# Weight sums of the second feed-forward layer as in-place adding transfers

## The chip, the cores and the metric

The kernel runs on one core of one Trainium2 chip. The metric is the device time of one execution in microseconds (us). The kernel before took 1249.65 us, the median of three runs that lie between 1248.87 and 1249.77 us.

## The reference, cut to what matters

One step of a decoder trunk of two layers: 512 prompt tokens and 64 sample tokens, width 1024, everything in float32. Layer 0 is a recurrent block, layer 1 windowed attention; each is followed by the feed-forward part that the change is about:

```
D_MODEL, D_FF = 1024, 2816
def swiglu(h, w_in, w_out):
    gate, up = jnp.split(h @ w_in, 2, axis=-1)
    return (jax.nn.silu(gate) * up) @ w_out
...
        h = modulate(rms_norm(x, norm_g[l, 1]), sh2, sc2)
        x = x + g2[:, None, :] * swiglu(h, ffn_w_in[l], ffn_w_out[l])
```

## The kernel before

**Halves and products.** The 576 tokens are handled as two halves of 288 columns, h = 0 and 1. A float32 product is made of three matmuls on operands that are split in a rounded part (`hi`, made by a cast on ScalarE) and the rest (`lo`, made by a subtraction on VectorE). `wh` are the ten buffers for split weights, `raw` the four buffers (512 KB each, 128 x 1024) into which weights are loaded by SyncE's queue, `h` the split input of the layer, `mm` the six PSUM banks.

**Pairs.** D_FF = 2816 is 22 blocks of 128 columns. The first three blocks of a layer (`PLAIN`) are computed directly. For each of the other 19 the gate's and the up projection's weight tile (a pair of `raw` tiles) are taken together as a 2 x 2 matrix of quarters r11, r12 (the gate tile's halves over the inner dimension) and r21, r22 (the up tile's), each 128 x 512, and the two halves of tokens as the other factor's columns. A Strassen scheme then needs seven products in place of eight: `11`, `12`, `22` take a plain quarter, `S1` to `S4` take sums of quarters. One product is 4 x 3 = 12 matmuls of 128x128 on 288 columns, a pair is 84.

**What stands where.** `steps(i)` gives seven closures for pair i; each calls `operand`, which claims a `wh` buffer, forms the sums that the product needs in place in the `raw` quarters (on VectorE), casts (ScalarE) and subtracts (VectorE). `todo` holds these closures in order, `pump` runs them as soon as `wh` buffers are left. `seven(i, name)` issues a product's matmuls and what follows them on PSUM. `raw.done()` gives a tile back, after which the next load may fill it. The blocks come in groups of 6, 6, 6 and 4 (the three plain ones are in the first); after a group its rows of `ffn_w_out` follow: `out(k, m, h)`, 8 x 2 products of 18 matmuls for a group of six.

**What sets the order.** Every call is recorded, and `Recorder.schedule` sorts all instructions of the whole program with costs of its own, then gives each engine its list, which that engine works off strictly in order. For a transfer issued by GpSimd (POOL) it reckons 1.02 us of issue, 0.65 us, 4 bytes per element at 345 bytes/ns, and 1.70 us, so 4.13 us from issue to landing for 128 x 512 floats. `reserve` says how many buffers of a kind must stay free when a tile is claimed out of turn; for `mm` it is 0.

The sums before, for one pair (r's are overwritten as they go):

```
S1:  r22 = r21 + r22
S2:  r21 = r11 - r21 ; r11 = r11 - r22
S4:  r12 = r12 - r11            (S3 takes r21)
```

Of the kernel before, what the change touches and what calls it, by code (L numbers as in the profile page):

```python
# [12 lines left out]
F32 = mybir.dt.float32  # L13
# [3 lines left out]
ALU = mybir.AluOpType  # L17
AX = mybir.AxisListType

P = 128  # L20
# [7 lines left out]
HC = 288  # L28
# [106 lines left out]
class Recorder:  # L135
    def __init__(self, shadow):
        self.shadow = shadow
        self.ops = []
        self.hist = {}
        self.kind_of = {}  # L140
        self.kinds = {}
        self.order = {}
        self.bias = 0
        self.hold = []
        self.batch = None
# [14 lines left out]
    def tile(self, pool, kind, cap, reserve, shape, dt, name):  # L160
        sh = self.shadow[kind in ("mm", "ada")].tile(shape, dt, tag=name, bufs=1, name="shadow_" + name)
        t = Sym(Ref(lambda: pool.tile(shape, dt, tag=kind, bufs=cap, name=name)), sh)
        n = sh.tensor.name
        self.kind_of[n] = kind
        self.kinds[kind] = (cap, reserve)
        self.order.setdefault(kind, []).append(n)
        return t

# [50 lines left out]
    def schedule(self):  # L219
# [35 lines left out]
        def alloc_time(op, now):  # L255
            t = 0.0
            need = {}
            for n in op.allocs:
                if n in got:
                    continue  # L260
                k = self.kind_of[n]
                sl = slots[k]
                i = need.get(k, 0)
                need[k] = i + 1
                o = self.order[k]
                while nxt[k] < len(o) and (o[nxt[k]] in got or o[nxt[k]] not in used):
                    nxt[k] += 1

                j, at = nxt[k], i
                while at and j + 1 < len(o):  # L270
                    j += 1
                    at -= o[j] not in got and o[j] in used
                m = i + (o[j] != n) * self.kinds[k][1]
                if len(sl) <= m:
                    return None
                t = max(t, sorted(sl)[m])
            return t
# [213 lines left out]
def trunk_kernel(ctx, tc, a):  # L491
# [10 lines left out]

    cnt = [0]

    def ps(pool=pmm, tag="mm"):
        cnt[0] += 1
        return rec.tile(pool, tag, NMM if tag == "mm" else (8 - NMM), RMM if tag == "mm" else 1, [P, 512], F32, f"{tag}{cnt[0]}")

    def aux():
        return ps()  # L510
# [401 lines left out]
    def quarters(c):  # L912

        if c == 0:
            kinds = [tb] * 8 + [ta] * 3 + [sl] * 13
            X2["kinds"] = kinds
            for j in (2, 3, 4):
                X2[j] = [None] * 4
        b11, b21, b12, b22 = [V2[h][k] for h, k in ((0, c), (0, c + 4), (1, c), (1, c + 4))]

        def two(j, y):
            X2[j][c] = [X2["kinds"].pop(0)(F32R) for _ in range(2)]
            split(X2[j][c][0].r[:, 0:HC], X2[j][c][1].r[:, 0:HC], y.f[:, 0:HC])
            y.done()

        def minus(o, p, q):
            V.tensor_tensor(*[y.f[:, 0:HC] for y in (o, p, q)], ALU.subtract)

        minus(b11, b12, b11)
        minus(b12, b22, b12)  # L930
        two(3, b12)
        minus(b22, b22, b11)
        minus(b21, b21, b22)
        two(2, b22)
        two(4, b21)

# [281 lines left out]
    def ffn(l, g, after):  # L1218
# [35 lines left out]
        todo = deque()  # L1254
        H2 = 4 * P

        def operand(i, name, src, sums=()):
            w = W[i, name] = whs()
            for o, p, q, op in sums:
                V.tensor_tensor(o, p, q, op)  # L1260
            S.copy(w.r[:, 0:H2], src)
            V.tensor_tensor(w.r[:, H2 : 2 * H2], src, w.f[:, 0:H2], ALU.subtract)

        def steps(i):

            ug_, uu = pairs_[i]

            def views():
                if uu.raw is None:
                    load_more()  # L1270
                return [u.raw.f[:, o : o + H2] for u in (ug_, uu) for o in (0, H2)]

            def a11():
                operand(i, "11", views()[0])

            def a22():
                operand(i, "22", views()[3])

            def s1():
                r11, r12, r21, r22 = views()  # L1280
                operand(i, "S1", r22, [(r22, r21, r22, ALU.add)])

            def s2():
                r11, r12, r21, r22 = views()
                operand(i, "S2", r11, [(r21, r11, r21, ALU.subtract), (r11, r22, r11, ALU.subtract)])

            def a12():
                operand(i, "12", views()[1])

            def s3():  # L1290
                operand(i, "S3", views()[2])
                uu.raw.done()
                nconv[0] += 1

            def s4():
                r11, r12, r21, r22 = views()
                operand(i, "S4", r12, [(r12, r12, r11, ALU.subtract)])
                ug_.raw.done()
                nconv[0] += 1

            return {"11": a11, "22": a22, "S1": s1, "S2": s2, "12": a12, "S3": s3, "S4": s4}

        def queue():
            for k, bs in enumerate(blocks):
                for i in range(max(PLAIN, sum(GROUPS[:k])), sum(GROUPS[: k + 1])):
                    st = steps(i)
                    if i == PLAIN:
                        nxt = steps(i + 1)
                        for s_, names in ((st, ("11", "12")), (nxt, ("11", "12")), (st, ("22", "S1", "S2", "S3", "S4")), (nxt, ("22", "S1", "S2", "S3", "S4"))):
                            for n in names:  # L1310
                                todo.append((1, s_[n]))
                    elif i > PLAIN + 1:
                        for n in ("11", "22", "S1", "S2", "12", "S3", "S4"):
                            todo.append((1, st[n]))
                for _ in {id(u) for u in outs[k][1]}:
                    todo.append((2, convert))
# [17 lines left out]
        def seven(i, name):  # L1334

            pump(lambda: (i, name) in W)
            w = W.pop((i, name))
            bank, ops = {"11": ("a", "B11"), "12": ("a", "B21"), "S1": ("e", "T1"), "S2": ("b", "T2"), "S3": ("b", "T3"),
                         "22": ("b", "T4"), "S4": ("e", "B22")}[name]
            b = B.setdefault(i, {})  # L1340
            if bank not in b:
                b[bank] = ps()
            o = b[bank][:, 0:HC]
            first = name in ("11", "S1", "S2")
            for k, (xh, xl) in enumerate(right(ops)):
                hi, lo = [w.r[:, q + k * P : q + (k + 1) * P] for q in (0, H2)]
                T.matmul(o, hi, xh, start=first and k == 0, stop=False, skip_group_check=True)
                T.matmul(o, hi, xl, start=False, stop=False, skip_group_check=True)
                T.matmul(o, lo, xh, start=False, stop=k == 3, skip_group_check=True)
            w.done()  # L1350
            pump()
            if name == "11":
                b["p1"] = ta()
                S.copy(b["p1"].f[:, 0:HC], o)
            elif name == "S1":
                b["p5"] = td()
                S.copy(b["p5"].f[:, 0:HC], o)
            elif name == "S2":

                V.tensor_tensor(o, o, b["p1"].f[:, 0:HC], ALU.add)  # L1360
                b["p1"].done()
                b["u2"] = td()
                S.copy(b["u2"].f[:, 0:HC], o)
            elif name == "12":

                b["g"] = ta()
                S.activation(b["g"].f[:, 0:HC], o, AF.Silu)
            elif name == "S3":

                y = b["p5"].f[:, 0:HC]  # L1370
                V.tensor_tensor(y, o, y, ALU.add)
            elif name == "22":

                y = b["g"].f[:, 0:HC]
                V.tensor_tensor(y, y, o, ALU.mult)
                whole(0, i, b["g"])
                del B[i]
            else:

                y, z = b["u2"].f[:, 0:HC], b["p5"].f[:, 0:HC]  # L1380
                V.tensor_tensor(y, o, y, ALU.add)
                S.activation(y, y, AF.Silu)
                G.tensor_tensor(z, y, z, ALU.mult)
                b["u2"].done()
                whole(1, i, b["p5"])
# [25 lines left out]
        def emit():  # L1411
            if l == 1:
                cache_out()
            queue()
            n_ = 0
            for k in range(len(GROUPS)):
                if k == 1 and l == 0:
# [30 lines left out]
                                ada_pace(1)  # L1448
                if k < len(GROUPS) - 1:
                    seven(n_, "11")  # L1450

        return emit

# [589 lines left out]
```

## Time and profile before

| what | value |
|---|---|
| median of three runs | 1249.65 us |
| span of the profiled execution (first to last instruction) | 1247.8 us |
| granted TensorE clock over the span | 0.994 |
| busy, of the span: TensorE / VectorE / ScalarE / GpSimd | 98% / 72% / 53% / 21% |
| moved by all transfers | 165.37 MB, mean 133 GB/s |

The span is that of one profiled execution; the page gives no other time for it, and the median lies 1.85 us above it. The second feed-forward layer runs from about 799 to 1238 us. Engine names in the profile: PE is TensorE, DVE VectorE, ACT ScalarE, POOL GpSimd, SPq and POOLq the queues of SyncE and GpSimd. All operations are recorded by one helper, so that all lines are L456 before and L458 after, and groups are told apart by tiles: `wh<-raw` is the making of a weight operand, `raw<-raw` a sum of quarters. "mean ns of one" is the time of one instruction; "idle before" is the time in which the engine stood still ahead of a group, with what ended it.

### The profile page before, as it was taken

The numbers are of one execution on the slowest core, as the hardware profiler recorded it, in microseconds if no ns is written. First come the engines' busy times: TensorE is split into PE (matmuls) and PEld (weight loads), VectorE is DVE, ScalarE is ACT, GpSimd is POOL, SyncE is SP. The second block draws the span as 40 slices with busy tenths as digits, with TensorE's granted clock in tenths as the row PEclk, the third lists the DMA queues.
The fourth block names the chain that finished last, engine by engine and source line by source line (L and its number), as shares of the span: only waits on it lengthen the run. The fifth ranks groups of instructions, "written<-read, shape, count | busy, mean of one in ns | idle before, by whom it ended". The sixth has DMA issues, their size and how long they took to land.

```text
span 1247.8 us, 25059 instructions
## 1 busy us (share of the span) xinstructions
PE 1225.9 (98%) x9468; PEld 1166.2 (93%) x9468; DVE 903.7 (72%) x2143; ACT 655.9 (53%) x1492; POOL 256.8 (21%) x542
## 2 busy tenths in 40 slices
PE   6999999999999999999999999999999999999997
PEld 4999999899999999999999888999999999999997
DVE  6789875984587467656779777658857856875776
ACT  4877773854155235423567578448523542552442
POOL 3455442100200110011034435100011011001011
PEclk8999999999999999999999999999999999999998
DMA  9966654434564654754612321422332332332322
GB/s 329 313 203 219 189 176 127 158 93 145 170 186 155 201 171 133 220 168 119 183 38 58 69 65 34 118 82 98 104 116 69 93 111 69 101 91 80 102 68 76
DMA packets 214507, 165.37 MB, mean 133 GB/s; under 512 B 23502, under 2 KB 197546, under 8 KB 214355
## 3 DMA queue, kind: packets, MB, share of 16 engines
q1 hardware_dynamic: 213938, 163.45, 43.0%
q8 instruction: 74, 1.21, 0.4%
q0 software_dynamic: 448, 0.32, 0.1%
q14 instruction: 47, 0.38, 0.1%
HBM read 160.85 MB, written 4.87 MB: 133 GB/s over the span
## 4 chain that ended last, share of the span: by engine, by line
PE 91%; ACT 3%; DVE 3%; DMA 2%; issue 1%; POOL 0%; SPq 0%; ACTq 0%; DVEq 0%; POOLq 0%
PE mm L456 86%; PE ada L456 5%; ACT ta L456 1%; DMA wh<-in_ada_w_dram 1%; ACT tb L456 1%; DMA raw<-in_rnn_w_in_dram 1%; DVE tb L456 0%; DVE h L456 0%; ACT h L456 0%; DVE sl L456 0%; DVE ta L456 0%; DVE wh L456 0%; SPq L456 0%; DVE acc L456 0%; ACT sl L456 0%
## 5 line engine op out<-in xcount | busy, mean ns | idle before, releaser
L456 PE MATMUL mm<-h,wh 128*128 128x288 f32 x4128 | 587.8, 297 | 1.5 <-ACT h L456 0.7
L456 PEld LDWEIGHTS mm<-h,wh 128*128 128x128 f32 x4128 | 558.4, 188 | 9.8 <-ACT h L456 2.5
L456 PE MATMUL mm<-sl,wh 128*128 128x288 f32 x3218 | 459.9, 296 | 0.0
L456 PEld LDWEIGHTS mm<-sl,wh 128*128 128x128 f32 x3218 | 436.6, 188 | 5.9 <-issue 3.4
L456 ACT CAST wh<-raw 128x512 fp32r<-128x512 f32 (+2 forms) x380 | 268.0, 722 | 325.2 <-PE mm L456 212.2
L456 DVE TENSOR_TENSOR wh<-raw,wh 128x512 fp32r<-128x512 f32 (+2 forms) x380 | 308.1, 825 | 73.5 <-ACT wh L456 50.1
L456 DVE SCALAR_TENSOR_TENSOR x<-mm,mods,x 128x256 f32<-128x256 f32 x160 | 76.9, 481 | 112.3 <-PE mm L456 112.2
L456 POOL TENSOR_TENSOR td<-td,td 128x288 f32<-128x288 f32 x38 | 35.5, 933 | 467.2 <-ACT td L456 461.1
L456 POOL TENSOR_TENSOR x<-x,ta 128x32 f32<-128x32 f32 x152 | 57.6, 380 | 309.2 <-DVE ta L456 309.1
L456 PE MATMUL mm<-tb,wh 128*128 128x288 f32 (+1 forms) x488 | 88.3, 297 | 0.0
L456 PEld LDWEIGHTS mm<-tb,wh 128*128 128x128 f32 x488 | 72.4, 188 | 1.9 <-DVE ta L456 0.8
L456 ACT COPY td<-mm 128x288 f32<-128x288 f32 (+2 forms) x140 | 49.0, 364 | 32.8 <-PE mm L456 16.8
L456 DVE TENSOR_TENSOR raw<-raw,raw 128x512 f32<-128x512 f32 x76 | 59.2, 779 | 0.5
L456 PE MATMUL mm<-ta,wh 128*128 128x288 f32 (+1 forms) x254 | 55.8, 297 | 0.0
L456 DVE TENSOR_TENSOR td<-mm,td 128x288 f32<-128x288 f32 x76 | 34.5, 454 | 25.9 <-PE mm L456 25.5
L456 ACT ACTIVATE ta<-x 128x288 f32<-128x288 f32 x56 | 24.4, 443 | 54.2 <-POOL x L456 51.1
L456 DVE TENSOR_TENSOR raw<-raw 128x512 f32<-128x512 f32 x76 | 52.1, 686 | 1.1
L456 PEld LDWEIGHTS mm<-ta,wh 128*128 128x128 f32 x254 | 41.7, 188 | 0.2
L456 PE MATMUL ada<-reg,cz 128*32 128x512 f32 (+1 forms) x304 | 36.1, 538 | 0.0
L456 ACT ACTIVATE ta<-ta,stat 128x256 f32<-128x256 f32 (+2 forms) x72 | 32.4, 475 | 7.0 <-DVE stat L456 6.8
L456 DVE TENSOR_TENSOR acc<-acc,ta 128x288 f32<-128x288 f32 x54 | 25.0, 464 | 13.6 <-ACT ta L456 13.3
L456 ACT CAST sl<-ta 128x288 fp32r<-128x288 f32 x54 | 23.2, 431 | 20.6 <-DVE ta L456 18.2
(201 smaller groups left out, 1195.0 us busy)
## 6 DMA issues: line engine op xcount, KB each, us to landing
raw<-in_ffn_w_in_dram SPq DMA_DIRECT2D x88, 512.0 KB
reg<-in_ada_w_dram SPq DMA_DIRECT2D x50, 512.0 KB
wh<-in_ada_w_dram SPq DMA_DIRECT2D x38, 512.0 KB
raw<-in_ffn_w_out_dram SPq DMA_DIRECT2D x48, 384.0 KB
raw<-in_rnn_w_in_dram SPq DMA_DIRECT2D x16, 512.0 KB
reg<-in_kv_ada_w_dram SPq DMA_DIRECT2D x10, 512.0 KB
raw<-in_rnn_w_out_dram SPq DMA_DIRECT2D x8, 512.0 KB
raw<-in_ffn_w_out_dram SPq DMA_DIRECT2D x8, 512.0 KB
```

Of the source, the lines that this page charges most:

```text
L456: self.rec.add(eng, lambda: getattr(obj, name)(*map(real, args), **{k: real(v) for k, v in kw.items()}), cost, outs, ins, func, lat, port, ...
```

## The change

The scheme is rewritten so that every sum of quarters is an addition into one of its own operands. The right factor's sums and the use of the products in PSUM take the signs that this leaves. In layer 0 the additions stay on VectorE (`plus` with l == 0), four per pair as before. In layer 1 each becomes a transfer issued from GpSimd with `accum_op=ALU.add`: 128 x 512 floats (256 KB) from one quarter added onto another, 76 in all for 19 pairs. The new sums of a pair, with the numbers that the prediction gives them:

```
(1) r11 += r21     after operand 11 has read r11
(2) r21 += r22     after (1)                      -> S1 reads r21
(3) r22 += r11     after (1), (2) and operand 22  -> S2 reads r22
(4) r12 += r22     after (3) and operand 12       -> S4 reads r12;  S3 reads r11, after (1)
```

The up tile is given back after (4), S1 and S2, the gate tile after S3 and S4. Two negations per pair (products `S3` and `22`) become scalar_tensor_tensor with a factor of -1 in place of tensor_tensor, in both layers, and so do two of the four differences of `quarters`. Last, in layer 1 the PSUM tiles `mm` are recorded with a reserve of 1 in place of 0 (`rmm`, `kept`).

```
+        def plus(o, p):
+            if l == 0:
+                V.tensor_tensor(o, o, p, ALU.add)
+            else:
+                G.dma_start(o, p, accum_op=ALU.add)
...
             def a22():
-                operand(i, "22", views()[3])
+                r11, r12, r21, r22 = views()
+                operand(i, "22", r22)
+                plus(r11, r21)
+                plus(r21, r22)
+                plus(r22, r11)
+                last_sum("22")
...
             def s2():
-                r11, r12, r21, r22 = views()
-                operand(i, "S2", r11, [(r21, r11, r21, ALU.subtract), (r11, r22, r11, ALU.subtract)])
+                operand(i, "S2", views()[3])
+                last_sum("S2")
...
+            def last_sum(name):
+                said.add(name)
+                if said >= {"22", "12"} and "sum" not in said:
+                    said.add("sum")
+                    plus(views()[1], views()[3])
+                if said >= {"sum", "S1", "S2"} and "up" not in said:
+                    said.add("up")
+                    uu.raw.done()
...
                 y = b["p5"].f[:, 0:HC]
-                V.tensor_tensor(y, o, y, ALU.add)
+                V.scalar_tensor_tensor(y, o, -1.0, y, ALU.mult, ALU.subtract)
...
+            rmm[0] = l
```

How this moves instructions is shown at two pairs in the middle of the layer, whose tiles are raw148 (gate) and raw149 (up), then raw150 and raw151. First VectorE before: three of the four sums of the first pair stand between its subtractions, and the fourth follows two rows on.

```order
L456 TENSOR_TENSOR wh401_12529<-raw149_12284,wh401_12529 128x512
L456 TENSOR_TENSOR x1_65<-x1_65,ta375_12536 128x32
L456 TENSOR_TENSOR raw149_12284<-raw149_12284 128x512
L456 TENSOR_TENSOR raw149_12284<-raw148_12232,raw149_12284 128x512
L456 TENSOR_TENSOR wh402_12556<-raw149_12284,wh402_12556 128x512
L456 TENSOR_TENSOR raw148_12232<-raw149_12284,raw148_12232 128x512
L456 TENSOR_TENSOR wh403_12579<-raw148_12232,wh403_12579 128x512
L456 TENSOR_TENSOR wh404_12585<-raw148_12232,wh404_12585 128x512
L456 TENSOR_TENSOR wh405_12592<-raw149_12284,wh405_12592 128x512
```

They are gone from VectorE, and POOL's list has them now. The same pair and the next one there, after the change, up to the first transfer of the two pairs that follow:

```order
L458 DMA raw148_12248<-raw149_12284 128x512
L458 DMA raw150_12515<-raw151_12534 128x512
L458 DMA raw149_12284<-raw149_12284 128x512
L458 DMA raw151_12534<-raw151_12534 128x512
L458 DMA raw149_12284<-raw148_12248 128x512
L458 TENSOR_TENSOR td137_12566<-td138_12590,td137_12566 128x288
L458 DMA raw151_12534<-raw150_12515 128x512
L458 DMA raw148_12248<-raw149_12284 128x512
L458 DMA raw150_12515<-raw151_12534 128x512
L458 TENSOR_TENSOR td139_12710<-td140_12756,td139_12710 128x288
L458 DMA raw152_12765<-raw153_12781 128x512
```

The two pairs' transfers alternate, (1) (1) (2) (2) (3) (3) (4) (4), and the gate-times-up product of the first pair (`td137`) stands among them. Over the whole layer the 19 pairs stand in 13 such runs: six runs of two pairs and, mostly where a group of blocks begins or ends, seven of one. ScalarE, in the list before, works the seven casts of the first pair (wh400 to wh406) nearly in a row, ahead of those of the second:

```order
L456 CAST wh400_12484<-raw148_12232 128x512
L456 CAST wh401_12529<-raw149_12284 128x512
L456 COPY ta376_12551<-mm451_12527 128x288
L456 CAST wh402_12556<-raw149_12284 128x512
L456 COPY td137_12570<-mm452_12548 128x288
L456 CAST wh403_12579<-raw148_12232 128x512
L456 CAST wh404_12585<-raw148_12232 128x512
L456 CAST wh405_12592<-raw149_12284 128x512
L456 ACTIVATE ta377_12607<-mm451_12527 128x288
```

In the list after, at the same place, the casts of the second pair (wh407, wh408, wh411, wh412) stand between those of the first, and S1's (wh402) comes behind six others:

```order
L458 CAST wh404_12570<-raw148_12248 128x512
L458 CAST wh407_12584<-raw150_12515 128x512
L458 COPY td138_12590<-mm453_12563 128x288
L458 ACTIVATE ta377_12603<-mm451_12523 128x288
L458 CAST wh408_12607<-raw151_12534 128x512
L458 COPY ta378_12621<-mm454_12599 128x288
L458 CAST wh405_12625<-raw148_12248 128x512
L458 CAST wh411_12639<-raw150_12515 128x512
L458 CAST wh412_12656<-raw150_12515 128x512
L458 CAST wh402_12663<-raw149_12284 128x512
```

So ScalarE's list, which also holds the copies out of PSUM (`ta<-mm`, `td<-mm`), now waits at several places for a transfer to land.

More of the change, by code (lines that the diff above doesn't have):

```diff
@@ L141, in __init__ @@
         self.kinds = {}
+        self.kept = {}
         self.order = {}
@@ L165, in tile @@
         self.kinds[kind] = (cap, reserve)
+        self.kept[n] = reserve
         self.order.setdefault(kind, []).append(n)
@@ L272, in alloc_time @@
                     at -= o[j] not in got and o[j] in used
-                m = i + (o[j] != n) * self.kinds[k][1]
+                m = i + (o[j] != n) * self.kept[n]
                 if len(sl) <= m:
@@ L503, in trunk_kernel @@
     cnt = [0]
+    rmm = [RMM]
     def ps(pool=pmm, tag="mm"):
         cnt[0] += 1
-        return rec.tile(pool, tag, NMM if tag == "mm" else (8 - NMM), RMM if tag == "mm" else 1, [P, 512], F32, f"{tag}{cnt[0]}")
+        return rec.tile(pool, tag, NMM if tag == "mm" else (8 - NMM), rmm[0] if tag == "mm" else 1, [P, 512], F32, f"{tag}{cnt[0]}")
     def aux():
@@ L927, in minus, with negated @@
             V.tensor_tensor(*[y.f[:, 0:HC] for y in (o, p, q)], ALU.subtract)
-        minus(b11, b12, b11)
+        def negated(o, p, q):
+            o, p, q = [y.f[:, 0:HC] for y in (o, p, q)]
+            V.scalar_tensor_tensor(o, p, -1.0, q, ALU.mult, ALU.subtract)
+        minus(b11, b11, b12)
         minus(b12, b22, b12)
         two(3, b12)
-        minus(b22, b22, b11)
-        minus(b21, b21, b22)
+        negated(b22, b22, b11)
+        negated(b21, b22, b21)
         two(2, b22)
@@ L1255, in ffn, with operand @@
         H2 = 4 * P
-        def operand(i, name, src, sums=()):
+        def plus(o, p):
[3 more added lines that the diff above has]
+                G.dma_start(o, p, accum_op=ALU.add)
+        def operand(i, name, src):
             w = W[i, name] = whs()
-            for o, p, q, op in sums:
-                V.tensor_tensor(o, p, q, op)
             S.copy(w.r[:, 0:H2], src)
@@ L1271, in views @@
                 return [u.raw.f[:, o : o + H2] for u in (ug_, uu) for o in (0, H2)]
+            said = set()
+            def last_sum(name):
[6 more added lines that the diff above has]
+                    uu.raw.done()
+                    nconv[0] += 1
+                if said >= {"S3", "S4"}:
+                    ug_.raw.done()
+                    nconv[0] += 1
             def a11():
@@ L1276, in a22 @@
             def a22():
-                operand(i, "22", views()[3])
+                r11, r12, r21, r22 = views()
[4 more added lines that the diff above has]
+                last_sum("22")
             def s1():
-                r11, r12, r21, r22 = views()
-                operand(i, "S1", r22, [(r22, r21, r22, ALU.add)])
+                operand(i, "S1", views()[2])
+                last_sum("S1")
             def s2():
-                r11, r12, r21, r22 = views()
-                operand(i, "S2", r11, [(r21, r11, r21, ALU.subtract), (r11, r22, r11, ALU.subtract)])
+                operand(i, "S2", views()[3])
+                last_sum("S2")
             def a12():
                 operand(i, "12", views()[1])
+                last_sum("12")
             def s3():
-                operand(i, "S3", views()[2])
-                uu.raw.done()
-                nconv[0] += 1
+                operand(i, "S3", views()[0])
+                last_sum("S3")
             def s4():
[L1296 to L1299, printed above, removed]
+                operand(i, "S4", views()[1])
+                last_sum("S4")
             return {"11": a11, "22": a22, "S1": s1, "S2": s2, "12": a12, "S3": s3, "S4": s4}
@@ L1370, in seven @@
                 y = b["p5"].f[:, 0:HC]
-                V.tensor_tensor(y, o, y, ALU.add)
+                V.scalar_tensor_tensor(y, o, -1.0, y, ALU.mult, ALU.subtract)
             elif name == "22":
                 y = b["g"].f[:, 0:HC]
-                V.tensor_tensor(y, y, o, ALU.mult)
+                V.scalar_tensor_tensor(y, o, -1.0, y, ALU.mult, ALU.mult)
                 whole(0, i, b["g"])
@@ L1450, in emit @@
                     seven(n_, "11")
+            rmm[0] = RMM
         return emit
```

## The prediction

> **What bounds the kernel now.** I first read the page's busy times, then the chain of waits in order of time, since it tells which engine ends each stage. The second feed-forward layer, the only place where transfers replace work, is one row of it:
>
> ```profile
> PE 1225.9 (98%) x9468; PEld 1166.2 (93%) x9468; DVE 903.7 (72%) x2143; ACT 655.9 (53%) x1492; POOL 256.8 (21%) x542
> ...
> 798.85 439.12 PE mm L456 x3311
> 1237.99 0.48 DVE x L456
> ```
>
> From 798.85 to 1237.99 us the chain never leaves PE. Then the windows, and the matmuls of that stretch by shape:
>
> ```profile
> 900.00:1000.00 100.00, 100.00 (x757) 100.00 (x756) 71.69 (x139) 42.68 (x86) 11.84 (x20) 1.00 0.33 96
> 820.00:860.00 40.00, 40.00 (x300) 39.39 (x299) 28.18 (x72) 25.33 (x63) 3.49 (x9) 1.00 0.35 113
> 940.00:980.00 40.00, 40.00 (x304) 40.00 (x303) 30.88 (x60) 18.50 (x39) 4.01 (x6) 1.00 0.28 80
> L456 PE MATMUL mm<-h,wh 128*128 128x288 f32 x1499 | 209.9, 296 | 0.1
> L456 PE MATMUL mm<-sl,wh 128*128 128x288 f32 x1417 | 204.7, 296 | 0.0
> ```
>
> The columns of a window are length, then busy us (and instructions) of PE, PEld, DVE, ACT, POOL, the granted clock, the share of the DMA engines, GB/s. PE starts 757 matmuls in 100 us at clock 1.00, one every 132.1 ns, and its idle time ahead of 2916 matmuls is 0.1 us. A pair's 84 matmuls take 84 x 132.1 ns = 11.1 us, an output part of 16 x 18 matmuls 38.0 us. VectorE, at 0.72, waits for PE. What VectorE loses here shortens nothing by itself.
>
> **What is taken away: 76 additions on VectorE.** The groups of 800 to 1237 us:
>
> ```profile
> L456 DVE TENSOR_TENSOR wh<-raw,wh 128x512 fp32r<-128x512 f32 (+2 forms) x170 | 129.6, 776 | 23.0 <-ACT wh L456 22.1
> L456 DVE TENSOR_TENSOR raw<-raw,raw 128x512 f32<-128x512 f32 x38 | 31.5, 830 | 0.2
> L456 DVE TENSOR_TENSOR raw<-raw 128x512 f32<-128x512 f32 x38 | 26.0, 687 | 0.5
> L456 ACT CAST wh<-raw 128x512 fp32r<-128x512 f32 (+2 forms) x170 | 113.8, 683 | 164.7 <-PE mm L456 95.2 <-DVE raw L456 41.9 <-issue 27.4
> ```
>
> 31.5 + 26.0 = 57.5 us of VectorE go, and with them the 41.9 us for which the casts waited for a sum. Both lie beside a PE that does not stand still. Worth: 0. The most that could be hidden in PE's even row is the difference between its best and its mean pace: 304 matmuls per 40 us are 131.6 ns each, the chain's 3311 take 132.6; 3311 x 1.0 ns = 3.3 us.
>
> **Signs, reserve, order.** 76 results in PSUM (two per pair, both layers) become scalar_tensor_tensor. The nearest rows:
>
> ```profile
> L456 DVE TENSOR_TENSOR td<-mm,td 128x288 f32<-128x288 f32 x38 | 17.3, 454 | 10.8 <-PE mm L456 10.8
> L456 DVE SCALAR_TENSOR_TENSOR x<-mm,mods,x 128x256 f32<-128x256 f32 x75 | 36.1, 481 | 62.1 <-PE mm L456 62.1
> ```
>
> 481 ns on 256 columns is at most 541 on 288, 87 more than 454; 76 x 87 ns = 6.6 us over both layers, on VectorE, which waits 62.1 us for PE in that one group of the second layer alone. The 16 negated differences (of `quarters`) add at most 16 x 87 ns = 1.4 us, on the same engine. Worth: 0; the cover is VectorE's waiting for PE, and if that were used up, the copies out of PSUM would be late next. In layer 0 the four additions per pair stay. The reserve and the new order put the same products in another sequence on PE; between -1 and +3 us, and I take +0.5: one missed matmul slot (0.13 us) at each of the four turns from pairs to outputs.
>
> **What is put in: 76 transfers of 256 KB, in series.** No transfer with an addition is in this trace, nor one from SBUF to SBUF. The nearest are POOL's own transfers in a stretch where the DMA engines are otherwise quiet, and one weight load:
>
> ```profile
> 229.25 1.14 POOL L456 DMA_DIRECT2D out_sample_conv_dram<-raw  x2
> 230.38 0.53 POOL L456 DMA_DIRECT2D out_prompt_conv_dram<-raw  x1
> 229.00:230.25 1.25, 1.25 (x11) 1.04 (x10) 0.95 (x4) 0.72 (x2) 1.11 (x3) 1.00 0.00 0
> 230.25:231.50 1.25, 1.25 (x12) 1.25 (x11) 1.25 (x5) 0.35 (x2) 1.25 (x4) 1.00 0.38 93
> 0.00:50.00 50.00, 39.03 (x372) 31.62 (x373) 32.28 (x101) 29.30 (x66) 15.74 (x39) 0.93 1.01 342
> DMA to landing us min/median/max: 1.9/2.9/3.9
> DMA to landing us min/median/max: 3.8/5.1/5.9
> 915.31 68.45 SPq L456 DMA_DIRECT2D raw<-in_ffn_w_in_dram  x12
> 915.00:916.25 1.25, 1.25 (x12) 1.25 (x11) 1.02 (x3) 0.12 (x1) 0.00 (x0) 1.00 0.00 0
> 916.25:917.50 1.25, 1.25 (x11) 1.25 (x11) 0.58 (x2) 0.00 (x0) 0.18 (x1) 1.00 0.67 196
> 917.50:918.75 1.25, 1.25 (x12) 1.25 (x11) 0.12 (x1) 0.20 (x1) 0.07 (x1) 1.00 0.74 223
> 918.75:920.00 1.25, 1.25 (x11) 1.25 (x11) 1.05 (x3) 0.63 (x1) 0.25 (x1) 1.00 0.00 0
> ```
>
> POOL is occupied 0.57 us by an issue (1.14 for two); the first bytes move 1.0 us after it (229.25, and 0 GB/s until 230.25). From issue to landing the two 48 KB transfers took 1.9 to 3.9, median 2.9 us (the first landing row); those at the program's start, of at most 48 KB with the DMA engines full (share 1.01 in the first 50 us, 342 GB/s), 3.8 to 5.9 (the second). The weight load of 512 KB, issued at 915.31, moves its bytes between 916.25 and 918.75: 210 GB/s with its run-up.
>
> L, from issue to landing of one addition: the 208 KB beyond 48 KB at 210 GB/s add 1.0 us to the median 2.9, so 3.9 us. The low end is 1.9 + 0.65 = 2.55 (the same bytes at about 330 GB/s, near the 342 of the first 50 us); the high end 3.9 + 1.0 + 1.25 = 6.15, if the quarter that is added onto has also to be read through the same engines at 210 GB/s. I take 3.9: the stretch has a DMA share of 0.33, nearer to the quiet rows than to the full ones.
>
> How long may L be? Transfers (1) to (4) of a pair wait for each other, two pairs alternate, and the next two pairs' tiles are loaded when these are given back. So one run on POOL's list costs: load to last byte 3.4 us (915.31 to 918.75 at most), its second tile 1.6 (0.52 MB at 330 GB/s), a cast 0.62 and a subtraction 0.69 (rows below) before (1), 4 L, and a cast and subtraction behind (4): 7.6 + 4 L.
>
> ```profile
> L456 ACT CAST wh<-raw x170: 605/622/1056, 803.2 to 1201.8; 128x512 fp32r<-128x512 f32 x133, 128x768 fp32r<-128x768 f32 x24, 128x1024 fp32r<-128x1024 f32 x13
> L456 DVE TENSOR_TENSOR wh<-raw,wh x170: 677/692/1473, 804.4 to 1203.5; 128x512 fp32r<-128x512 f32 x133, 128x768 fp32r<-128x768 f32 x24, 128x1024 fp32r<-128x1024 f32 x13
> ```
>
> PE has 2 x 11.1 = 22.2 us of work for it: L may be (22.2 - 7.6)/4 = 3.65. Over a group of six pairs, four runs share 6 x 11.1 + 38.0 = 104.6 us: (26.15 - 7.6)/4 = 4.64, if the output part's own weights cost the buffers nothing. I put the limit in the middle, 4.15 us. With L = 3.9 the transfers are hidden, by a quarter of a microsecond. Beyond the limit each microsecond costs up to 13 runs x 4 = 52 us, since ScalarE's list stops at the cast that waits (S1's behind (2), S2's behind (3)), behind it the copies that empty PSUM, and behind those PE; POOL's list stops too, with the `td` products that the output part needs. SyncE's next loads come only after (4).
>
> A sentence of the Trainium skill speaks against my 3.9: "Collectives: The Full Stack", section "The bandwidth ceiling", says that an addition in the DMA engines needs two source reads on the same ring, which halves its rate. No run here shows it yet; by it the second read's 1.25 us would be added, L = 5.15 and (5.15 - 4.15) x 52 = 52 us more than before.
>
> **Sum.** Against the profiled execution: span 1247.8 + 0 (VectorE) + 0 (signs) + 0.5 (order) + 0 (transfers, hidden) = 1248.3 us. The median of the runs lies 1.85 us above this span; with it 1250.1 us. About 0.2% (2.5 us) is what a measurement of this kernel can tell from no change.
>
> **Rivals.**
>
> *Landings longer than the cover (slower).* Everything as above, with L from 4.2 us up. It decides where L passes 4.15; at 4.65 it costs 26 us (1276), at 5.15 52 us (1302), at 6.15 104 us (1354). For it speaks that 3.65 to 4.64 straddles my own L, that pairs alternate, so two additions share the DMA engines, and that the start's landings took 3.8 to 5.9 us. Against: they stood in a DMA share of 1.01, and the 0.33 here is mostly loads that wait for (4) themselves.
>
> *POOL kept from issuing by VectorE (slower).* POOL's own products in this layer vary:
>
> ```profile
> L456 POOL TENSOR_TENSOR td<-td,td x19: 802/1034/1344, 896.4 to 1205.8; 128x288 f32<-128x288 f32 x19
> ```
>
> From 0.80 to 1.34 us: a neighbour costs up to 0.54 us. If an issue suffers the same, L = 4.44 and (4.44 - 4.15) x 52 = 15 us, 1265. The Trainium skill ("SBUF — State Buffer", section "Who interferes with whom") has such a lock for descriptors, but only beside VectorE's copies, casts and tensor_scalar operations; the groups above are tensor_tensor, so by that page this does not happen here. No run shows either.
>
> *Something is gained (faster).* PE's pace of 132.6 ns hides small stalls, such as the 300 matmuls in 820 to 860 us against 304 later. If VectorE's freed 57.5 us remove them all, the 3.3 us of above go: 1246.4. Against it: the slower windows lie in the direct blocks and the first pairs, where the sums are fewest, and the trace may lack a few records.
>
> **Chances.** Hidden, 1247.5 to 1253: 0.52 (0.45 of it within 0.2%, 0.05 slower, 0.02 faster). Landings too long: 0.33. POOL kept from issuing: 0.07. Gain: 0.08. So faster 0.10, same 0.45, slower 0.45. The range of all cases, 1246 to 1290, leaves out L above some 4.9 us, about 0.13, and a gain above the 3.3 us.
>
> **What the profile after would show.** If right: the page's VectorE falls from 903.7 to about 850 us; 76 transfers `raw<-raw` from POOL, 256 KB, about 3.9 us to landing; the chain still one PE row of some 440 us; casts `wh<-raw` waiting for transfers without PE waiting for casts. If landings are too long: PE's digits fall below 9 from the 27th slice on, PE waits for `wh` of ACT and DVE, several us per run of POOL's list, 13 such places; SyncE's loads issued later in each run. What makes me wrong most easily is L: I have no row of an addition, and a quarter of a microsecond decides.

## The result, and the profile after

The changed kernel takes 1258.0 us (median of four runs, 1257.02 to 1259.76) against 1249.26 for the kernel before on the same chips: ratio 1.0072, with a 95% interval of 1.0058 to 1.0087. It is slower by 8.7 us, inside the range, but not the likeliest case, which was "no change". The profiled execution took 1257.02 us with a span of 1255.0 us and a granted clock of 0.995, as before.

The page after, busy times, queues and the new issues:

```profile
PE 1228.2 (98%) x9468; PEld 1166.2 (93%) x9468; DVE 849.0 (68%) x2067; ACT 656.6 (52%) x1492; POOL 320.6 (26%) x618
...
q1 hardware_dynamic: 213938, 163.45, 43.0%
q0 software_dynamic: 11392, 20.25, 9.7%
...
raw<-raw POOLq DMA_DIRECT2D x76, 256.0 KB, 3.5
```

VectorE fell from 903.7 to 849.0 us and 76 transfers of 256 KB are there, as predicted. They land sooner than predicted, after 3.5 us in the median against 3.9. Still PE needs longer. The windows over the whole second feed-forward layer of both kernels (columns as in the prediction) say how:

```profile
798.85:1238.00 439.15, 439.15 (x3313) 437.66 (x3313) 316.92 (x679) 197.47 (x412) 46.78 (x93) 1.00 0.31 91
```

and after:

```profile
798.73:1244.60 445.87, 441.64 (x3313) 438.27 (x3313) 264.71 (x602) 198.74 (x412) 110.15 (x169) 1.00 0.58 134
```

The layer is 6.7 us longer with the same 3313 matmuls at the same clock: PE stood still for 4.2 us (445.87 - 441.64; before 0), and its busy time grew by 2.5 us. The rest of the 7.2 us by which the spans differ is 0.6 us behind the layer. The chain of waits after, which was one row before, has breaks:

```profile
798.73 97.45 PE mm L458 x726
...
897.96 3.45 DMA raw<-raw
901.45 0.49 issue
901.94 6.04 DMA raw<-raw
908.00 0.63 ACT wh L458
908.67 83.67 PE mm L458 x629
992.37 0.40 ACT td L458
992.77 0.53 ACT wh L458
993.34 13.10 PE mm L458 x96
...
1008.61 4.93 DMA raw<-in_ffn_w_out_dram
1013.56 1.36 ACT wh L458 x2
1014.97 84.26 PE mm L458 x632
1099.25 0.40 ACT td L458
1099.65 0.53 ACT wh L458
...
1211.60 0.41 ACT td L458
```

The breaks at 908, at 1015 and from 1211 to 1218 lie where work turns from pairs to an output part. Those at 993 and 1100 lie within runs of two pairs, whose transfers POOL issues from 979.58 to 995.45 and from 1087.17 to 1102.55. What PE waits for in the layer:

```profile
PE mm L458 <- ACT wh L458: 2.7, 4, 0.9
PE mm L458 <- ACT td L458: 1.0, 1, 1.0
PE mm L458 <- ACT sl L458: 0.5, 1, 0.5
```

(us in total, times, longest.) Always ScalarE. Two kinds of break are seen. At 908 and 1015 a transfer or a load landed late. At 992 and 1099 no transfer is in the chain: ScalarE's list has a copy out of PSUM, which waits for PE, ahead of a cast that PE needs next. (At 1211 and 1217 no transfer is in the chain either; PE waits there for the last pair's copies and for the cast of its product.) The timelines of POOL and ScalarE at 992, in the kernel after:

```profile
987.99 1.77 POOL L458 DMA_DIRECT2D raw<-raw  x2
992.37 0.40 ACT L458 COPY td<-mm 128x288 f32<-128x288 f32 x1 [2.19 <-PE mm L458]
992.67 0.62 ACT L458 CAST wh<-raw 128x512 fp32r<-128x512 f32 x1
```

The cast is S1's of the second of two pairs. The transfer that it needs, the first of POOL's two, was issued at 987.99 and landed after 3.3 us, at 991.3. The cast starts 1.4 us after that, when the copy has got its product, though ScalarE had been idle for 2.19 us, and PE starts again at 993.34, 0.87 us late.

### The profile page after: what moved, and what is told of

Its sections match the earlier page's. It is cut to its first block, busy times and chain, and to the rows that moved or that the text cites. A ratio compares the mean times of both kernels' runs of the same rounds, so it can differ in the third digit from the quotient of the medians.

```text
span 1255.0 us, 25159 instructions
## 1 busy us (share of the span) xinstructions
PE 1228.2 (98%) x9468; PEld 1166.2 (93%) x9468; DVE 849.0 (68%) x2067; ACT 656.6 (52%) x1492; POOL 320.6 (26%) x618
## 3 DMA queue, kind: packets, MB, share of 16 engines
q1 hardware_dynamic: 213938, 163.45, 43.0%
q0 software_dynamic: 11392, 20.25, 9.7%
## 4 chain that ended last, share of the span: by engine, by line
PE 88%; ACT 4%; DVE 3%; DMA 3%; issue 1%; POOL 0%; SPq 0%; ACTq 0%; DVEq 0%; POOLq 0%
PE mm L458 84%; PE ada L458 5%; ACT ta L458 1%; DMA wh<-in_ada_w_dram 1%; ACT tb L458 1%; DMA raw<-raw 1%; DMA raw<-in_rnn_w_in_dram 1%; DVE wh L458 1%; DVE tb L458 0%; DVE h L458 0%; DVE sl L458 0%; ACT wh L458 0%; ACT h L458 0%; DVE ta L458 0%; DMA raw<-in_ffn_w_out_dram 0%
## 5 line engine op out<-in xcount | busy, mean ns | idle before, releaser
L458 POOL DMA_DIRECT2D raw<-raw x76 | 66.5, 890 | 139.9 <-DMA raw<-raw 71.5
L458 DVE TENSOR_TENSOR raw<-raw,raw 128x512 f32<-128x512 f32 x57 | 39.7, 697 | 0.3
L458 DVE TENSOR_TENSOR mm<-mm,ta 128x288 f32<-128x288 f32 x38 | 17.5, 462 | 25.5 <-PE mm L458 25.4
L458 ACT ACTIVATE td<-td 128x288 f32<-128x288 f32 x38 | 16.9, 444 | 33.5 <-DVE td L458 33.5
```

What stands on the lines that cost most here:

```text
L458: self.rec.add(eng, lambda: getattr(obj, name)(*map(real, args), **{k: real(v) for k, v in kw.items()}), cost, outs, ins, func, lat, port, ...
```

## The experiments

Two theories: **landings** (the transfers' data come too late for the casts) and **lists** (the order in which the planner puts the instructions, because it reckons with 4.13 us per transfer, costs PE time whether the data are late or not). Beside them stood the signs and the reserve. All kernels start from the changed one, and each was compared with the kernel before on its own chip (1248.98 to 1249.22 us).

### First four: what part costs what

**`short`**: the transfers cut to 64 of their 512 columns with every list unchanged; 7/8 of each sum is left out. Recorded as one operation with its old costs:

```
+        if name == "dma_start" and "accum_op" in kw:
+            def emit():
+                o, p = map(real, args)
+                for c0, c1 in [(0, 64)]:
+                    obj.dma_start(o[:, c0:c1], p[:, c0:c1], **kw)
+            self.rec.add(eng, emit, cost, outs, ins, func, lat, port, mode)
+            return
```

> Every instruction stands where it does in the changed kernel; only each adding transfer is cut to the first 64 of its 512 columns (seven eighths of every sum are left out), so that it should land in some 2.5 us in place of 3.5 (3.3 to 6.3). Order theory (the lists were sorted for landings of 4.13 us, and the casts that PE waits for stand too late in ScalarE's list whatever the transfers do): 8.7 us slower than before stays nearly whole, +6 to +9 us. Collision theory (PE waits where a transfer lands late beside weight loads, 6.0 us at 901.94): most of it goes, +0 to +3 us.

Measured: 1255.27 us, +6.05 (ratio 1.0049, 1.0036 to 1.0062). The landings of `short`:

```profile
DMA to landing us min/median/max: 2.1/2.2/5.0
```

With landings 1.3 us shorter than after's 3.5, only 2.7 of the 8.7 us came back. The window over its layer:

```profile
798.04:1242.10 444.06, 440.80 (x3313) 438.29 (x3313) 264.44 (x602) 195.83 (x412) 109.62 (x169) 1.00 0.38 95
```

and what PE waits for there:

```profile
PE mm L465 <- ACT wh L465: 1.7, 2, 0.9
PE mm L465 <- ACT td L465: 1.0, 1, 1.0
PE mm L465 <- ACT sl L465: 0.5, 1, 0.5
```

The `td` and `sl` waits are those of after, to the tenth; of the four `wh` waits two are gone. Its chain shows which:

```profile
798.04 192.67 PE mm L465 x1444
990.74 0.40 ACT td L465
991.13 0.53 ACT wh L465
991.70 105.53 PE mm L465 x791
```

and its timeline of ScalarE what stands at 991:

```profile
990.74 0.40 ACT L465 COPY td<-mm 128x288 f32<-128x288 f32 x1 [2.18 <-PE mm L465]
991.03 0.62 ACT L465 CAST wh<-raw 128x512 fp32r<-128x512 f32 x1
```

The breaks at 908 and 1015 are gone, so they were the landings. That at 992 stands there with the same 2.18 us of an idle ScalarE, although the transfer that its cast needs had landed at 988.5: it is the list.

**`dve`**: the sums on VectorE in both layers, with the new signs, places and reserve (`if l == 0` in `plus` made `if True`).

> The sums stay additions into their own operand with turned signs and the reserve of 1, but in both layers on VectorE; no adding transfer is left. Order theory and collision theory both: back to before, -1 to +1 us. If signs, the new places of the sums or the reserve carried the loss: +3 to +9 us.

Measured: 1250.12 us, +0.9 (1.0009, 1.0000 to 1.0018). Its layer:

```profile
798.65:1239.26 440.61, 440.14 (x3314) 438.32 (x3314) 310.97 (x678) 199.04 (x413) 46.32 (x93) 1.00 0.30 90
```

PE stands still for 0.5 us. Signs, places and reserve together cost 0.9 us (by the interval, 0 to 2.2). `short` is 5.2 us slower than `dve` and has no transfer in its chain of this layer: that is what the lists cost that are built around transfers.

**`res0`**: `rmm[0] = l` made `rmm[0] = 0`.

> The changed kernel with the PSUM reserve of the second layer back at 0. If the reserve costs PE its stand-ins at the turns from pairs to outputs: back to +3 us or less. Order theory and collision theory (the reserve plays no part): +8 to +9.5 us, as the changed kernel.

Measured: 1258.21 us, +9.0 (1.0070, 1.0057 to 1.0084). That is the changed kernel's time: the reserve does nothing that can be measured.

**`two`**: each sum in two transfers of 256 columns, lists unchanged (the edit of `short` with `[(0, 256), (256, 512)]`).

> Same lists as in the changed kernel, but each adding transfer is issued as two of 256 columns each, one behind the other, so that a sum lands about one more issue (0.87 us) later, at 4.3 to 4.5 us. My prediction's limit of 4.15 us with 52 us for each us beyond it: 10 to 20 us on top of the changed kernel, +18 to +29 us against before. Order theory with plenty of cover left: no more than +2 us on top, +9 to +11 us.

Measured: 1261.23 us, +12.0 (1.0100, 1.0086 to 1.0113). A piece lands after 3.4 us in the median. The second is issued 0.6 us behind the first, and a sum is there 4.4 us after its first issue (medians of the 76 sums in the trace). 0.9 us more than after cost 3.3 us: no cliff at 4.15. The PE waits of `two`:

```profile
PE mm L465 <- ACT wh L465: 5.1, 6, 1.1
PE mm L465 <- ACT td L465: 1.0, 1, 1.0
```

Later data lengthen the `wh` waits alone; the list's `td` wait stays at 1.0.

### Second four: the time that the planner is told

If the lists cost by what the planner reckons with, then another figure gives another loss. The term for the landing was changed for these transfers alone, first by 1000 ns down or up (3.13 and 5.13 us in place of 4.13):

```
-... n * 4 / (250.0 if pk <= 512 else 308.0 if pk <= 1024 else 345.0) + 5
+... n * 4 / (250.0 if pk <= 512 else 308.0 if pk <= 1024 else 345.0) + 5 + (-1000 if "accum_op" in kw else 0)
```

**`plan_m1_short`**: told 3.13 us, transfers of 64 columns (7/8 of each sum left out, as in `short`).

> The planner is told that an adding transfer lands in 3.13 us (1 us less than it reckoned), so it sorts the lists anew; the transfers are cut to 64 of 512 columns (seven eighths of every sum left out), which land in 2.2 us. Order theory (the 6.1 us that short transfers still cost are the price of lists spread out for landings of 4.13 us): the PE waits of 0.9 to 1.0 us at the turns go, -1 to +3 us against before. If the loss sits in having four landings in a row at all, or in POOL's list, whatever is reckoned: +5 to +7 us, as with short transfers and the old lists.

Measured: 1251.07 us, +2.0 (1.0019, 1.0010 to 1.0028). Of the 6.05 us of `short`, 4.0 are gone, with the same transfers.

**`plan_m1`**: told 3.13 us, whole transfers.

> The planner is told 3.13 us, the transfers are whole and land in 3.4 us or more, and a step of the chain with the next issue takes 4.0. Order theory: closer lists leave too little for the real landings, PE waits at many places, +10 to +40 us. If the reckoned landing were only a wasted allowance: less than the changed kernel, 0 to +6 us.

Measured: 1322.8 us, +73.7 (1.0592, 1.0577 to 1.0606), far more than expected. They land after 3.4 us in the median, 0.3 us later than told. What PE waits for:

```profile
PE mm L458 <- ACT td L458: 31.1, 13, 3.1
PE mm L458 <- DVE td L458: 15.1, 7, 4.7
```

Not for weights, but for the products that ScalarE and VectorE should have taken out of PSUM. ScalarE's casts `wh<-raw` waited 156.5 us for transfers into `raw`, in 64 waits, where after has 37.9 us in 27; the copies stand behind them in the list. This is the way that the prediction gave for landings beyond the cover, set off by a list without room. But waits are not all of it. The window over this layer:

```profile
798.65:1309.00 510.35, 462.87 (x3310) 456.57 (x3311) 270.60 (x602) 197.13 (x413) 107.76 (x169) 0.96 0.50 117
```

PE stood still for 47.5 us, and its busy time is 23.7 us longer than before (439.15), at a granted clock of 0.96 where it was 1.00. 439.15/0.96 is 457, so the clock makes up some 18 us of that, as an estimate. Why it was lower, no run tests.

**`plan_p1`**: told 5.13 us, whole transfers.

> The planner is told 5.13 us, the transfers are whole and land in 3.5 us (6 at most). Order theory: each us reckoned more spreads the lists further and PE pays for it though every landing is in time, +10 to +16 us against before. Collision theory as the main cause (late landings cost, allowance protects): less than the changed kernel, +2 to +7 us.

Measured: 1269.17 us, +20.1 (1.0162, 1.0148 to 1.0176). More room than the median landing needs (3.8; the longest took 5.8) makes it slower still.

**`only4`**: only sum (4) of a pair as a transfer, 19 in all, none waiting for another; the others on VectorE.

```
-        def plus(o, p):
-            if l == 0:
+        def plus(o, p, far=False):
+            if l == 0 or not far:
...
-                    plus(views()[1], views()[3])
+                    plus(views()[1], views()[3], True)
```

> Only the last sum of each pair (r12 += r22, for S4) is a transfer in layer 1, 19 in all; the other three are additions on VectorE. One landing per pair in place of four in a row. If the loss goes with the number of landings in series: a quarter of 8 us, about +1 to +3 us. If one waiting cast per pair is enough to break ScalarE's list: +5 to +8 us.

Measured: 1252.3 us, +3.2 (1.0025, 1.0015 to 1.0035). Fewer transfers, less loss; but even these do not gain on VectorE's additions.

### Last four: which of the two, and how it goes in between

**`plan_p1_short`**: told 5.13 us, transfers of 64 columns (7/8 of each sum left out). The one run that tells the theories apart at the far end: by landings +20 should vanish, by lists it should stay.

> The planner is told 5.13 us as in the kernel that took 20.1 us more than before, and the transfers are cut to 64 of 512 columns (seven eighths of every sum left out). Order theory: landings in 2.2 us help nothing, +17 to +20 us. If late landings still had a part at 5.13 us reckoned: below +12 us.

Measured: 1267.19 us, +18.2 (1.0146, 1.0132 to 1.0161). It stayed. The PE waits of `plan_p1`:

```profile
PE mm L458 <- ACT td L458: 7.0, 6, 1.3
PE mm L458 <- ACT ta L458: 2.0, 4, 0.5
```

and of `plan_p1_short`, with landings of 2.2 us in place of 3.8:

```profile
PE mm L465 <- ACT td L465: 7.0, 6, 1.3
PE mm L465 <- ACT ta L465: 2.0, 4, 0.5
```

Same waits, same sums: PE here waits for the lists and not for data.

**`plan_p025` and `plan_m025`**: told 4.38 and 3.88 us, whole transfers.

> The planner is told 4.38 us, whole transfers. Order theory in its simple form (each us reckoned beyond what the transfers need costs PE some 11 us, from 8.7 at 4.13 to 20.1 at 5.13): +10 to +13 us against before. If what costs is not the allowance but where one sort happens to leave a copy ahead of a cast at the turns: anything from 0 to +10 us, and PE waits at other places than at the changed kernel's four turns.

> The planner is told 3.88 us, whole transfers, whose step in the chain takes 3.98. Simple order theory: between the changed kernel and the one told 3.13 (+74 us), where real landings begin to be late: +5 to +25 us. One sort's chance: 0 to +12 us.

Measured: 1254.15 us, +5.2 (1.0044, 1.0030 to 1.0058), and 1263.49 us, +14.5 (1.0115, 1.0101 to 1.0130). A quarter of a microsecond more room gains 3.5 us on the changed kernel, a quarter less loses 5.8. In `plan_p025` PE's waits are down to 1.8 us, though its transfers land later (3.9 in the median). The two rows that are not shown have 0.3 and 0.2 us:

```profile
PE mm L458 <- DVE wh L458: 1.0, 2, 0.8
PE mm L458 <- ACT td L458: 0.3, 1, 0.3
```

The idea behind the second four, a loss that grows evenly with the room given, is wrong between 4.13 and 4.38.

**`three`**: each sum in three transfers (171, 171 and 170 columns), lists unchanged.

> Lists of the changed kernel, each sum issued as three transfers of 171, 171 and 170 columns, so that it lands two issues (1.8 us) later, at some 5.2 us. My prediction's price, 52 us for each us over 4.15: (5.2 - 4.15) x 52 = 55 us against before, +45 to +75 us. A price of that of two pieces carried on (3.3 us for the first 0.9): +15 to +20 us.

Measured: 1292.1 us, +43.1 (1.0347, 1.0332 to 1.0361). The PE waits of `three`:

```profile
PE mm L465 <- ACT wh L465: 19.8, 17, 2.7
```

The third piece is issued 1.1 us after the first and lands after 4.4 us, and a sum is there 5.8 us after its first issue (medians of the 76 sums in the trace). POOL is also full in the runs of two pairs; its timeline has

```profile
963.35 10.79 POOL L462 DMA_DIRECT2D raw<-raw  x12 [2.57 <-DVE wh L465]
```

At 0.9 us each, 24 issues are 21.6 us of the 22.2 us that PE has for two pairs. Of the 43 us PE stood still for 25.3 in this layer, and its busy time grew by 16.5 at a clock of 0.99. How the loss divides between late sums and a full POOL stays open.

All of it in one table, us over the kernel before:

| told to the planner | 3.13 | 3.88 | 4.13 | 4.38 | 5.13 |
|---|---|---|---|---|---|
| whole transfers (land 3.4 to 3.9) | +73.7 | +14.5 | +8.7 | +5.2 | +20.1 |
| 64 columns (land 2.2) | +2.0 | | +6.1 | | +18.2 |

The lower row is the price of the lists that the planner made for that room, the upper has on top what the landings cost with the same lists: 72 us at 3.13, 2.7 at 4.13, 1.9 at 5.13. With whole transfers the least that was seen is +5.2. No version that was run beats the kernel before.

## Why the prediction was right and wrong

**The time lies in the range by luck.** 1258.0 us is none of the cases as they were worked out: the likeliest ended at 1253, and the rival with long landings needed L above 4.15 us, where the median was 3.5. The time came into the range because a term that I had bounded by +3 us, the order, cost about 6.

**What is taken away, worth 0: right.** VectorE gave up 54.7 us (903.7 to 849.0) and no kernel gained by it. The rival "something is gained" is out.

**Signs and reserve, worth 0: right,** within the 0.9 us of `dve`, whose interval begins at 1.0000, and `res0`.

**Order, +0.5 us, between -1 and +3: this step failed.** `short`, with data that are there early, costs +6.05 us; all but the 0.9 of `dve` is the order with transfers in it. I had reckoned one matmul slot of 0.13 us at each of four turns. In `short` PE stops four times and waits 3.3 us: 0.87 us at 991 and again at 1097, both within runs of two pairs, and 1.0 and 0.5 us at the last turn. (Its layer is 4.9 us longer in all; 1.7 of that is PE's longer busy time.) The first two stops are a cast that the planner put behind a copy out of PSUM. The order that the prediction's own document quotes showed such casts moved behind others; I read from it that products change places, and not that ScalarE's strict list ties a cast to an unrelated copy.

**Transfers, hidden, 0: wrong by 2.7 us,** the difference of after and `short`. L itself was 3.5 us where I took 3.9, within 2.55 to 6.15, and a link of two transfers, from issue to next issue, took 3.98 us in the chain (897.96 to 901.94). The steady part has less cover than worked out: the eight transfers of a run of two pairs take 21.8 us after, from the issue at 953.08 to the last landing at 974.89 (18.5 to 22.1 us in the six such runs), where 4 L gave 15.6, against PE's 22.2. Still no transfer is in the chain within these runs. The tail was not in the sum: the landing of 6.04 us at 901.94 came while the output part's weight loads were running. Three windows of one microsecond around it:

```profile
902.00:903.00 1.00, 1.00 (x10) 1.00 (x9) 0.96 (x3) 0.18 (x2) 0.81 (x1) 1.00 0.07 20
904.00:905.00 1.00, 1.00 (x10) 1.00 (x9) 1.00 (x2) 0.00 (x0) 0.42 (x1) 1.00 1.16 261
907.00:908.00 1.00, 0.96 (x8) 0.72 (x6) 0.00 (x0) 0.18 (x1) 0.00 (x0) 1.00 0.12 32
```

and the loads' row in the timeline of SyncE's queue:

```profile
893.26 17.39 SPq L458 DMA_DIRECT2D raw<-in_ffn_w_out_dram  x5
```

The DMA engines go from a share of 0.07 to more than full (1.16) and back to 0.12 before the transfer counts as landed. That they are shared with the loads is seen, and an addition fills them even alone (the second read, below); which packet held the last one up is not seen.

**The limit of 4.15 us and 52 us per microsecond beyond it: both too steep.** 4.4 us (`two`) cost 3.3 us more than after where (4.4 - 4.15) x 52 gives 13; 5.8 us (`three`) cost 34 us more than after where it gives 86, and there POOL was full too. That not every late cast stops PE would fit this, but no run tests it. Where lists are packed closer (`plan_m1`) the price is as steep as I had it, 72 us for 1.2 us more of landing or 60 us per us, though part of that is the lower clock. So the limit belongs to the list and not to the kernel: it moves with what the planner is told.

**The rivals.** "Landings longer than the cover" had the sign right; by its own terms (L above 4.15) it did not happen in the median, though 17 of the 76 landings took longer. "POOL kept from issuing by VectorE" did not happen. POOL's row among the operations on the weight tiles, and their landings, in the kernel after:

```profile
L458 POOL DMA_DIRECT2D raw<-raw x76: 861/874/1206, 874.2 to 1208.3; - x76
DMA to landing us min/median/max: 3.3/3.5/6.3
```

An issue takes 874 ns in the median beside VectorE's tensor_tensor operations. The longest, about 1.2 us, are those that begin while the issue before them still runs (958.87 and 959.42, for one). The Trainium skill ("SBUF — State Buffer", section "Who interferes with whom") names copies, casts and tensor_scalar operations as what can keep descriptors waiting, and not tensor_tensor; the trace agrees for tensor_tensor, with these numbers.

**The second read.** The Trainium skill ("Collectives: The Full Stack", section "The bandwidth ceiling") has the add of a reduce-scatter at half the rate of a copy, since it needs two source reads. The trace bears it out for the additions here. A stretch of the kernel after in which queue q0 alone moved data, as a window and as the queue's row:

```profile
899.60:900.90 1.30, 1.30 (x12) 1.30 (x11) 0.05 (x1) 1.30 (x4) 0.00 (x0) 1.00 1.01 173
q0 software_dynamic: 124, 0.23, 100.8%
```

One addition fills all 16 DMA engines (share 1.01) at 173 GB/s; the transfers of the first 50 us, for the most part loads, moved 342 GB/s at the same share. Over the whole execution, by the queue rows of the page, q0 moved 20.25 MB in 9.7% of 16 x 1255.0 us, 10.4 GB/s per engine, the loads of q1 18.9 GB/s (163.45 MB in 43.0%), a factor of 1.8. The time to landing goes with it: 224 KB more take 1.3 us (3.5 against 2.2), about 175 GB/s. The 5.15 us that I had worked out by that rule were too long because I put the second read on top of 210 GB/s, which is one load with its run-up and not the rate of full engines.

**What stays open:** why 4.38 us gives a better list than 4.13. Only one set of lists was made for each figure, so how much of a difference is the room, and how much the one sort that came of it, is not separated. Open too is most of the 2.5 us by which PE's busy time in the layer grew without a recorded wait (1.7 in `short`, 8.7 in `plan_p1`). About 1.0 of the 2.5 comes with the six stops, as an estimate: a matmul's record lasts 297 ns, but in an even row the next one starts after 132, so each stop costs some 0.16 us more than the wait that is shown.

## What to carry to other kernels

When a short operation on an engine with time to spare becomes a transfer of several microseconds, its cost is not only whether the data come in time: a strict list per engine needs room planned for the latency, and that room ties unrelated operations (here a cast behind a PSUM copy) to the transfer's schedule. Here that cost the bound engine time even when the data were early. To tell the two apart, shrink the transfer with all lists unchanged, then change the planned latency with the transfer unchanged. Where the bound engine never stands still, as in this layer, freeing another engine gains nothing, and what is put in its place has only losses to give.

## What the runs showed of the hardware that I had not expected

- A transfer that adds 256 KB within SBUF lands 3.5 us after its issue (3.3 to 6.3), one of 32 KB after 2.2 (2.1 to 5.0): 224 KB more take 1.3 us, about 175 GB/s.
- Such a transfer alone fills the 16 DMA engines (share 1.01) at 173 GB/s, half of the 342 GB/s that the transfers of the first 50 us reach at that share.
- POOL is occupied 0.87 us by an issue of such a transfer, whether it moves 256 KB or 32 KB (874 ns after, 876 in `short`), against 0.57 us for the 48 KB transfers of the kernel before. The next issue can start 0.55 us after it (958.87 and 959.42 after), but in a long row one comes every 0.9 us (`three`).
- Cut in pieces, a sum comes later and not sooner: 256 KB as two transfers are there after 4.4 us, as three after 5.8.
- The granted clock was lower where PE stopped often: 0.96 over the layer in `plan_m1`, 0.99 in `three`, against 1.00 before.
